# Scan loads placed over the convolution's buffers, with a lasting weight slot, fewer copies and evenly spread preparation steps

## The chip, the cores and the metric

The kernel runs on one core of one Trainium2 chip. A core has a matrix engine (PE, with its weight loads shown as PEld), a vector engine (DVE), a scalar engine (ACT), GpSimd (POOL) and a sync engine (SP) that here only issues transfers. Each engine works through its own instructions in the order fixed when the kernel is built, and waits where an instruction's inputs or its buffer are not ready. The metric is the device time of one execution in microseconds. Three runs of the kernel before took 1540.7, 1546.32 and 1547.51 us; their median is 1546.32.

## The reference

One layer of a diffusion backbone over 1024 latent tokens and 256 context tokens of width 1024. Cut to its course:

```python
px = modulate(rms_norm(x, norm1_w[i]), sh1, sc1) @ w_in[i]
pc = modulate(rms_norm(ctx, norm1_w[i]), csh1, csc1) @ w_in[i]
dn_c, s_ctx_f, s_ctx_b = gated_deltanet(pc[..., :DN_IN], ..., s_zero, s_zero)
dn_x, _, _ = gated_deltanet(px[..., :DN_IN], ..., s_ctx_f, s_ctx_b)
qx, kx, vx = na_qkv(px[..., DN_IN:], ...)
qc, kc, vc = na_qkv(pc[..., DN_IN:], ...)
na_x = neighborhood_attention(qx, kx, vx, kc, vc, na_rpb[i], rows)
x = x + g1 * (jnp.concatenate([dn_x, na_x], axis=-1) @ w_out[i])
x = x + g2 * swiglu(modulate(rms_norm(x, norm2_w[i]), sh2, sc2), w_ffn_in[i], w_ffn_out[i])
```

`gated_deltanet` convolves q, k and v over the sequence (five taps, then SiLU), normalises q and k, and runs a gated delta rule in chunks, forward and backward, each over the context first. Its output is normalised per head and multiplied by `silu(z)`. `neighborhood_attention` gives each latent query one softmax over a clamped 8 x 16 window of keys and all context keys.

## The kernel before

The work goes through four stages: the normalised, modulated tokens; the input projection as a list of jobs; the two scans, with the attention filled in between their steps; and the output projection with the feed-forward part, which holds more than half of the time and is not touched.

**Order.** Only the first stage's order is written out by hand. Everywhere else the program is built from Python generators, and the framework's scheduler orders the instructions of each engine when the kernel is built: by the place in the program, and by when it expects inputs and buffers to be ready. Its expectations are not the chip's times; the chip then keeps the order. SP's queue of transfers is ordered in the same way.

**The job list** (L1030 to L1039) is k0 to k3, z1, nk0 to nk2, nv0, nk3, q0 to q3, nq0 to nq3, v0, nv1, v1 to v3, z0. A `Block` (k, q, v with convolution; nk, nq without) computes 128 output columns for all tokens: eight steps of matmuls with split operands hh and hl (L405), then the evacuation by ACT into a raw tile `cr` (L453), the taps on DVE into `cacc` (L457, L461), SiLU on ACT (L468), and, one or two jobs later, `norm` and `finish`. For v, `finish` transposes `cacc` on PE (L527), scales it on DVE into `vt` (L531), and SP stores it to v_d (L535). For nk and nq, `norm` multiplies the squares with a block of ones in two or three segments (L492), each followed by Ln on ACT (L493), with two PSUM banks of the name "m". A `Wide` job (z, nv) takes 256 columns with the tokens as stationary operand (L595), tile by tile; its weights come in two halves through a single raw buffer `wraw` (load L586, cast on ACT L587, remainder on POOL L588) into a tile `zw`. z1, nv0 and nv1 take `zw` from a pool `zp` on the left side; z0 takes a tile of its own from a pool `sp1`, made where `zp`, `adp` and the preparation's pools have been closed. z0 writes its gate tiles `zg` into slots of the tag "kx" and stores them from ACT (L627). While z0 runs, PSUM is divided anew: it then has two banks for everything beside the attention.

**Beside the jobs** two backgrounds advance: `block_inverses` and `preps` (the chunks' triangular inverses and decay tables, kk, at, y), and `modulation`. A Block gives the first of them one step for each of its eight matmul steps, a Wide job two for each tile, and nv1 three. What is left is drained at the beginning of v3. The preparation's results go out by SP (L1010) to at_d and y_d, and its decay matmuls read the masks `mr` and a constant `mneg` (L968).

**Around the change's middle.** After nv1, SP copies the latent values within DRAM into the window layout vw_d, in 64 transfers of 32 rows (L1108). At the beginning of v3 the attention's pool `nw` is made and its first loads are issued: queries, keys (L260 to L263), context values, bias tiles (cleared by POOL, L271) and window values. The attention's generator `fill` is then advanced during z0 and the scans.

**The right side of the memory** is a stack of pools: the projection's weights `wpb`, the operands hh and hl in `hp` and `hp2`, and the convolution's pool `cp` (cacc, cr, kx, zt). After the last job it is reused in the same order by `wpf`, `arp`, then `sl` (three buffers of each of the scans' loads but v), a spacer, and `sw` (the scans' working tiles, and v). So `sl` lies mostly over the last of the operands hh and hl, and `sw` mostly over `cp`. The scans' loads are L1165; their first matmul is L1217.

Of the kernel before, what the change touches and what calls it, by code (L numbers as in the profile page):

```python
# [20 lines left out]
KT = 8  # L21
# [67 lines left out]
def hybrid(ctx, tc, a, dbg):  # L89
# [47 lines left out]
    mr = const("mr", [128, 5, 128], F32R)  # L137
    mneg = const("mneg", [128, 2, 128], F32R)

# [235 lines left out]
    with ExitStack() as bs:  # L375
# [32 lines left out]
        class Block:  # L408
# [64 lines left out]
            def norm(self):  # L473
# [8 lines left out]
                if kind == "q":  # L482
# [6 lines left out]
                    return  # L489
                for s0, n in self.segs:  # L490
                    p = bank()
                    pe.matmul(p[:, :n], M[C_BD2], r[:, s0:s0 + n], start=True, stop=True)  # L492
                    act.activation(r[:, s0:s0 + n], p[:, :n], AF.Ln, bias=b_eps, scale=1.0 / ND)  # L493
# [26 lines left out]
            def finish(self):  # L520
                kind, acc, i = self.kind, self.acc, self.i
                if kind in "kv":
                    vt = cp.tile([128, NCH, 128], F32, name="vt", tag="kx", bufs=3)
                    for g, m in ((0, 4), (4, 4), (8, 2)):
                        p = bank()
                        for c in range(m):
                            pe.transpose(p[:, c * 128:(c + 1) * 128], acc[:, (g + c) * 128:(g + c + 1) * 128], ident)  # L527
                        if kind == "k":
                            act.copy(vt[:, g:g + m].rearrange("p c d -> p (c d)"), p[:, :m * 128])
                        else:  # L530
                            dve.tensor_tensor(vt[:, g:g + m], p[:, :m * 128].rearrange("p (c d) -> p c d", d=128),  # L531
                                              SV[:, g:g + m, i:i + 1].to_broadcast([128, m, 128]), OP.mult)
                        yield
                    dst = v_d if kind == "v" else k_d
                    sp.dma_start(dst[:, i * 128:(i + 1) * 128].rearrange("(c p) d -> p c d", p=128), vt)  # L535
                if kind == "q":
# [27 lines left out]
        class Wide:  # L564


            def __init__(self, kind, half, zp):
                self.kind, self.half, self.zp = kind, half, zp
                self.n = 272 if kind == "z" and half else 256
                self.lasting = kind == "z" and not half  # L570

            def room(self):
                w = self.zp().tile([128, 2, KT, 256 if self.lasting else 272], F32R, name="zw", tag="zw")
                self.hi, self.lo = w[:, 0], w[:, 1]

            def prefetch(self):
                h2, n = 2 * self.half, self.n // 2
                src = a["w_nv"] if self.kind == "nv" else a["w_z%d" % self.half]
                if self.kind == "z":
                    h2 = 0  # L580
                if not self.lasting:
                    self.room()
                for i in range(2):
                    raw = wp.tile([128, KT, 136], F32, name="wraw", tag="wraw", bufs=1)
                    r, s = raw[:, :, :n], slice(i * n, i * n + n)
                    sp.dma_start(r, src[h2 + i])  # L586
                    act.copy(self.hi[:, :, s], r)  # L587
                    pool.tensor_tensor(self.lo[:, :, s], r, self.hi[:, :, s].bitcast(F32), OP.subtract)  # L588
# [10 lines left out]
            def tiles(self):  # L599
# [18 lines left out]
                for t in range(2, NCH):  # L618
                    p = self.wide(t, 0, self.n)
                    if half == 0:  # L620
                        if t % 4 == 2:
                            zg = cp.tile([128, NCH, 128], F32, name="zg", tag="kx", bufs=3)
                            zg = zg.rearrange("p a b -> p (a b)")[:, :1024]
                        act.copy(zg[:, (t - 2) % 4 * 256:(t - 2) % 4 * 256 + 256], p[:, :256])
                        if t % 4 == 1:
                            act.activation(zg, zg, AF.Silu)
                            act.dma_start(z_d[(t - 5) * 128:(t - 1) * 128, 0:256].rearrange("(c p) d -> p c d", p=128),  # L627
                                          zg.rearrange("p (c d) -> p c d", d=256))
                        yield
                        continue  # L630
# [13 lines left out]
        with ExitStack() as xs:  # L644
# [65 lines left out]
            with tc.manual_schedule(engines={mybir.EngineType.PE, mybir.EngineType.DVE, mybir.EngineType.Activation}):  # L710
# [30 lines left out]
                for k in range(1, KT):  # L741
# [12 lines left out]
                    if k == 5:  # L754
                        act.copy(mr[:, 4], ident)
                        for d in range(2):
                            act.mul(mneg[:, d], masks[:, d], -1.0e30)
                        act.copy(mr[:, 0:4], masks)

        cp = pools(bs, "cp", "right")  # L760
        late = ExitStack()
        adp = pools(late, "adp", "left")
        zpool = [pools(late, "zp", "left")]
        first_half = ExitStack()
        cpa = pools(first_half, "cpa", "left")
        WK = cpa.tile([128, 2, NU, 32], F32, name="WK", tag="WK")
        KKc = WK[:, 1]

        def zp():
            return zpool[0]  # L770

# [53 lines left out]
        def block_inverses():  # L825
            with ExitStack() as gs:
# [55 lines left out]
                for c in range(30, 0, -1):  # L882
# [5 lines left out]
                    if c % 2:  # L888
                        yield
                flat = N.rearrange("p b r c -> p b (r c)")  # L890
                dve.memset(flat[:P, :, 0:1024:33], 1.0)
# [137 lines left out]

        jobs = first + [Block("k", 2), Block("k", 3), Wide("z", 1, zp)]  # L1030
        inv = len(jobs)
        jobs += [Block("nk", i) for i in range(3)] + [Wide("nv", 0, zp), Block("nk", 3)]
        turn = len(jobs)
        jobs += [Block("q", i) for i in range(4)]
        later = len(jobs)
        queries = range(turn, later)
        jobs += [Block("nq", i) for i in range(4)] + [Block("v", 0), Wide("nv", 1, zp)]
        values = len(jobs) - 1
        jobs += [Block("v", i) for i in (1, 2, 3)] + [Wide("z", 0, zp)]  # L1039

# [11 lines left out]
        for n in range(2, len(jobs) + 2):  # L1052
# [7 lines left out]
            if n == len(jobs) - 2:  # L1060
                bg.drain()
                bg2.drain()
                late.close()
                sp1 = pools(middle, "sp1", "left")
                zpool[0] = sp1
                jobs[n + 1].room()
                fill = attention(pools(attn, "nw", "left", 2))
                next(fill)
# [8 lines left out]
            if isinstance(j, Wide):  # L1077
                for t, _ in enumerate(j.tiles()):
# [4 lines left out]
                    if t == 4 and nrm:  # L1083
# [5 lines left out]
                        nrm = None  # L1089
                    bg.step(3 if n == values else 2)  # L1090
            elif j:
                for k in range(KT):
                    j.mm([k])
                    if k >= 3:
                        next(fin, 0)
                    bg.step(1)
                    if n > inv + 4:
# [5 lines left out]
            if isinstance(j, Wide) and n == values:  # L1103
                vlat = nv_d[CT:].rearrange("(r c) d -> r c d", c=64)
                for cb in range(4):
                    for ch in range(4):
                        for r in range(4):
                            sp.dma_start(vw_d[r * 32:r * 32 + 32, :, cb, ch],  # L1108
                                         vlat[4 * ch + r, BLKS[cb]:BLKS[cb] + 32].rearrange("c (h d) -> c h d", d=128))
            if nrm:  # L1110
# [30 lines left out]

    with ExitStack() as gs:
        sl = pools(gs, "sl", "right", 3)
        shift(gs, "spad", "right", 16)
        sw = pools(gs, "sw", "right", 2)
        gs.callback(scan_psum.close)
# [14 lines left out]
        def load(d, c, near):  # L1161

            def tile_of(name, src):
                t = work(name, 3) if name == "v" else sl.tile([128, 4, 128], F32, name=name, tag=name)
                sp.dma_start(fl(t), src)  # L1165
# [612 lines left out]
```

## Time and profile before

| | us |
|---|---|
| median of three runs | 1546.32 |
| lowest, highest | 1540.7, 1547.51 |
| the profiled execution | 1549.54 |
| its span in the profile | 1547.5 |
| PE busy in it | 1479.8 |
| DVE, ACT, POOL busy | 994.3, 727.7, 233.6 |

The jobs run to about 595 us of the span, the scans with the attention to about 815, the output projection and the feed-forward part to the end. The profile gives, for each group of instructions, its line, engine, operation and operands, its count, busy time and mean duration, and the idle time of its engine just before it with what ended that idle time. Names like PEq, ACTq, SPq are an engine's queue of transfers and other instructions that do not compute. A strip of 40 digits cuts the span into equal slices of 38.7 us. In a list in order of time the first column is the start, the second the duration, and a bracket at the end tells how long the engine had stood and what released it.

### The profile page before, as it was taken

What the parts mean: (1) busy time and instruction counts of PE and PEld (TensorE: products, weight loads), DVE (VectorE), ACT (ScalarE), POOL (GpSimd) and SP (SyncE); (2) the same over time, 40 slices, a digit from 0 to 9 for tenths busy, and PEclk for the clock granted to TensorE, in tenths of its full rate; (3) what the DMA queues carried; (4) which work ended last, traced back from release to release, by engine and by line L of the source; (5) the groups of instructions that cost most, each with busy time, mean ns of one, the idle gap of its engine ahead of it and who ended that gap; (6) DMA issues with size and microseconds to landing.
All of it is one profiled execution on the core that took longest, in us unless ns stands there. A gap on an engine that the chain in (4) does not pass through costs nothing. (4 is left out here: it accounts for less than half of the span.)

```text
span 1547.5 us, 23963 instructions
## 1 busy us (share of the span) xinstructions
PE 1479.8 (96%) x8702; PEld 1235.2 (80%) x8702; DVE 994.3 (64%) x1712; ACT 727.7 (47%) x1404; POOL 233.6 (15%) x286
## 2 busy tenths in 40 slices
PE   6999999899989978999999999999999999999998
PEld 3788787678778867888887878888888888888887
DVE  5774497675554543777986469866665556599652
ACT  5442552635764235666773166333333334354440
POOL 1154500733554010111210000000000000000000
PEclk9999999999999979999999999999999999999999
DMA  9274221577556467899637502632323324698742
GB/s 389 64 217 133 67 72 63 163 212 241 182 169 212 130 174 237 283 288 261 220 102 255 208 34 82 211 102 103 103 102 103 109 100 159 231 381 279 244 144 82
DMA packets 204118, 267.35 MB, mean 173 GB/s; under 512 B 16736, under 2 KB 114528, under 8 KB 202976
## 3 DMA queue, kind: packets, MB, share of 16 engines
q1 hardware_dynamic: 198480, 261.07, 51.7%
q10 hardware_dynamic: 5520, 4.76, 0.9%
q8 instruction: 68, 1.11, 0.3%
q14 instruction: 50, 0.41, 0.1%
HBM read 201.02 MB, written 68.94 MB: 174 GB/s over the span
## 5 line engine op out<-in xcount | busy, mean ns | idle before, releaser
L405 PE MATMUL blk<-hh,whi 128*128 128x512 f32 (+1 forms) x410 | 123.4, 395 | 2.3 <-ACT kk L550 1.4
L1415 ACT CAST uhi<-wq 128x512 fp32r<-128x512 f32 x101 | 61.0, 622 | 133.5 <-issue 84.6
L1415 ACT CAST uhi<-ws 128x512 fp32r<-128x512 f32 x91 | 53.9, 621 | 147.3 <-PE ps L1354 92.9
L405 PE MATMUL blk<-hl,whi 128*128 128x512 f32 (+1 forms) x410 | 116.8, 377 | 0.3 <-DVE hl L707 0.3
L595 PE MATMUL blk<-zw,hh 128*128 128x256 f32 (+1 forms) x576 | 115.0, 293 | 1.3 <-ACT kk L550 1.1
L405 PE MATMUL blk<-hh,wlo 128*128 128x512 f32 (+1 forms) x410 | 114.7, 377 | 0.6 <-POOL wlo L200 0.6
L1416 DVE TENSOR_TENSOR ulo<-wq,uhi 128x512 fp32r<-128x512 f32 x101 | 67.4, 687 | 59.1 <-ACT uhi L1415 34.0
L1354 PE MATMUL ps<-hT,uhi 128*128 128x512 f32 x336 | 103.7, 390 | 0.0
L1354 PE MATMUL ps<-hT,ulo 128*128 128x512 f32 x336 | 103.5, 389 | 0.0
L1354 PE MATMUL ps<-lT,uhi 128*128 128x512 f32 x336 | 103.4, 389 | 0.0
L595 PEld LDWEIGHTS blk<-zw,hh 128*128 128x128 f32 x576 | 92.8, 192 | 5.2 <-ACT kk L550 1.4
L1354 PE MATMUL ps<-hB,uhi 128*128 128x512 f32 x288 | 89.2, 391 | 0.6 <-ACT hB L1529 0.6
L1354 PE MATMUL ps<-lB,uhi 128*128 128x512 f32 x288 | 88.7, 389 | 0.4 <-DVE lB L1530 0.4
L1354 PE MATMUL ps<-hB,ulo 128*128 128x512 f32 x288 | 88.7, 389 | 0.0
L405 PEld LDWEIGHTS blk<-hh,wlo 128*128 128x128 f32 x410 | 72.6, 192 | 15.3 <-POOL wlo L200 0.9
L405 PEld LDWEIGHTS blk<-hl,whi 128*128 128x128 f32 x410 | 72.4, 191 | 14.5 <-DVE hl L707 0.8
L405 PEld LDWEIGHTS blk<-hh,whi 128*128 128x128 f32 x410 | 69.4, 194 | 18.2 <-issue 4.5
L595 PE MATMUL blk<-zw,hl 128*128 128x256 f32 (+1 forms) x288 | 83.2, 289 | 0.0
L1354 PEld LDWEIGHTS ps<-lT,uhi 128*128 128x128 f32 x336 | 63.1, 188 | 13.1
L1354 PEld LDWEIGHTS ps<-hT,ulo 128*128 128x128 f32 x336 | 63.1, 188 | 13.1
L1354 PEld LDWEIGHTS ps<-hT,uhi 128*128 128x128 f32 x336 | 62.9, 188 | 13.0
L200 POOL TENSOR_TENSOR wlo<-wraw,whi 128x1024 fp32r<-128x1024 f32 x18 | 44.7, 2485 | 179.2 <-ACT whi L199 160.7
(359 smaller groups left out, 3540.5 us busy)
## 6 DMA issues: line engine op xcount, KB each, us to landing
wq<-w_fo SPq DMA_DIRECT2D x99, 256.0 KB, 4.2
wq<-w_gu SPq DMA_DIRECT2D x88, 256.0 KB, 2.9
wad<-wa SPq DMA_DIRECT2D x64, 256.0 KB, 4.4
bt<-rpb SPq DMA_DIRECT2D x64, 192.0 KB, 3.8
t_d<-g SPq DMA_DIRECT2D x22, 512.0 KB, 3.6
fr<-t_d SPq DMA_DIRECT2D x44, 256.0 KB, 5.0
f_d<-g SPq DMA_DIRECT2D x33, 256.0 KB, 2.1
fr<-f_d SPq DMA_DIRECT2D x33, 256.0 KB, 3.8
```

What stands on the lines that cost most here:

```text
L200: lo_engine.tensor_tensor(o, r, h.bitcast(F32), OP.subtract)
L405: pe.matmul(o, ww[:, k], xx[k][:, s], start=k == 0 and j == 0, stop=k == KT - 1 and j == 2)
L595: pe.matmul(p[:, :c1 - c0], x[k][:, s], ww[:, k, c0:c1], start=k == 0 and j == 0, stop=k == KT - 1 and j == 2)
L1354: pe.matmul(o, w[wi][:, k], x[xi][:, k], start=first and k == 0 and j == 0, stop=k == n - 1 and j == 2, skip_group_check=True)
L1415: act.copy(hi, self.raw[key])
L1416: dve.tensor_tensor(lo, self.raw[key], hi.bitcast(F32), OP.subtract)
```

## The change

Eight edits, told apart:

1. **vw_d**: 16 transfers of 4 x 32 rows in place of 64 of 32 rows.
2. **v_d stores** are issued by ACT in place of SP.
3. **The weight slot**: `sp1` is made at the beginning and lasts; all Wide jobs take `zw` from it, z0 too. `zp` is gone.
4. **mneg** moves out of the constants into `adp`, and is made from `mr` after the first stage.
5. **norm**'s third segment takes a bank of the name "pr", the preparation's pair.
6. **Gate tiles** `zg` take a slot of the raw tiles' tag "cr" in place of "kx".
7. **Steps**: nv1 gives two per tile, as other Wide jobs; Blocks from nq0 on give ten in place of eight; `block_inverses` has two empty steps more before it sets the diagonal.
8. **The scans' pools** change places: `sw` first, `sl` last, and v's three buffers move to `sl`. So `sl` lies over `cp`, and `sw` over the last of the operands.

```diff
-    mneg = const("mneg", [128, 2, 128], F32R)
...
-                for s0, n in self.segs:
-                    p = bank()
+                for j, (s0, n) in enumerate(self.segs):
+                    p = bank("pr" if j == 2 else "m")
...
-                    sp.dma_start(dst[:, i * 128:(i + 1) * 128].rearrange("(c p) d -> p c d", p=128), vt)
+                    (act if kind == "v" else sp).dma_start(dst[:, i * 128:(i + 1) * 128].rearrange("(c p) d -> p c d", p=128), vt)
...
-                self.lasting = kind == "z" and not half
...
-                w = self.zp().tile([128, 2, KT, 256 if self.lasting else 272], F32R, name="zw", tag="zw")
+                w = sp1.tile([128, 2, KT, 272], F32R, name="zw", tag="zw")
...
-                if not self.lasting:
-                    self.room()
+                self.room()
...
-                            zg = cp.tile([128, NCH, 128], F32, name="zg", tag="kx", bufs=3)
-                            zg = zg.rearrange("p a b -> p (a b)")[:, :1024]
+                            zg = cp.tile([128, T], F32, name="zg", tag="cr", bufs=2)
+                            zg = zg[:, :1024]
...
-                        for d in range(2):
-                            act.mul(mneg[:, d], masks[:, d], -1.0e30)
                         act.copy(mr[:, 0:4], masks)
...
         late = ExitStack()
+        sp1 = pools(middle, "sp1", "left")
         adp = pools(late, "adp", "left")
-        zpool = [pools(late, "zp", "left")]
+        mneg = adp.tile([128, 2, 128], F32R, name="mneg", tag="mneg")
+        for d in range(2):
+            act.mul(mneg[:, d], mr[:, d].bitcast(F32), -1.0e30)
...
                     if c % 2:
                         yield
+                yield
+                yield
                 flat = N.rearrange("p b r c -> p b (r c)")
...
                 late.close()
-                sp1 = pools(middle, "sp1", "left")
-                zpool[0] = sp1
-                jobs[n + 1].room()
...
-                    bg.step(3 if n == values else 2)
+                    bg.step(2)
...
-                    bg.step(1)
+                    bg.step(1 + (n >= later and k in (2, 6)))
...
-                        for r in range(4):
-                            sp.dma_start(vw_d[r * 32:r * 32 + 32, :, cb, ch],
-                                         vlat[4 * ch + r, BLKS[cb]:BLKS[cb] + 32].rearrange("c (h d) -> c h d", d=128))
+                        sp.dma_start(vw_d[:, :, cb, ch].rearrange("(r c) h d -> r c h d", c=32),
+                                     vlat[4 * ch:4 * ch + 4, BLKS[cb]:BLKS[cb] + 32].rearrange(
+                                         "r c (h d) -> r c h d", d=128))
...
-        sl = pools(gs, "sl", "right", 3)
-        shift(gs, "spad", "right", 16)
         sw = pools(gs, "sw", "right", 2)
+        shift(gs, "spad", "right", 16)
+        sl = pools(gs, "sl", "right", 3)
...
-                t = work(name, 3) if name == "v" else sl.tile([128, 4, 128], F32, name=name, tag=name)
+                t = sl.tile([128, 4, 128], F32, name=name, tag=name)
```

More of the change, by code (lines that the diff above doesn't have):

```diff
@@ L564, in hybrid, with __init__ @@
         class Wide:
-            def __init__(self, kind, half, zp):
-                self.kind, self.half, self.zp = kind, half, zp
+            def __init__(self, kind, half):
+                self.kind, self.half = kind, half
                 self.n = 272 if kind == "z" and half else 256
-                self.lasting = kind == "z" and not half
             def room(self):
-                w = self.zp().tile([128, 2, KT, 256 if self.lasting else 272], F32R, name="zw", tag="zw")
+                w = sp1.tile([128, 2, KT, 272], F32R, name="zw", tag="zw")
                 self.hi, self.lo = w[:, 0], w[:, 1]
@@ L767, in hybrid @@
         KKc = WK[:, 1]
-        def zp():
-            return zpool[0]
         def decay_tables(gp):
@@ L1028, in preps @@
                 flush(tick[0] + 2)
-        jobs = first + [Block("k", 2), Block("k", 3), Wide("z", 1, zp)]
+        jobs = first + [Block("k", 2), Block("k", 3), Wide("z", 1)]
         inv = len(jobs)
-        jobs += [Block("nk", i) for i in range(3)] + [Wide("nv", 0, zp), Block("nk", 3)]
+        jobs += [Block("nk", i) for i in range(3)] + [Wide("nv", 0), Block("nk", 3)]
         turn = len(jobs)
@@ L1036, in hybrid @@
         queries = range(turn, later)
-        jobs += [Block("nq", i) for i in range(4)] + [Block("v", 0), Wide("nv", 1, zp)]
+        jobs += [Block("nq", i) for i in range(4)] + [Block("v", 0), Wide("nv", 1)]
         values = len(jobs) - 1
-        jobs += [Block("v", i) for i in (1, 2, 3)] + [Wide("z", 0, zp)]
+        jobs += [Block("v", i) for i in (1, 2, 3)] + [Wide("z", 0)]
         def blk(n):
@@ L1142, in hybrid @@
     with ExitStack() as gs:
+        sw = pools(gs, "sw", "right", 2)
+        shift(gs, "spad", "right", 16)
         sl = pools(gs, "sl", "right", 3)
-        shift(gs, "spad", "right", 16)
-        sw = pools(gs, "sw", "right", 2)
         gs.callback(scan_psum.close)
```

## The prediction

> **What bounds the kernel now.** I read the page first, for which engine is full and where its clock drops; then the busy time of single stretches; then the matrix engine in order of time; then the queues that feed it.
>
> ```profile
> span 1547.5 us, 23963 instructions
> PE 1479.8 (96%) x8702; PEld 1235.2 (80%) x8702; DVE 994.3 (64%) x1712; ACT 727.7 (47%) x1404; POOL 233.6 (15%) x286
> PE   6999999899989978999999999999999999999998
> PEclk9999999999999979999999999999999999999999
> ```
>
> PE is busy 96% of the span, so the change, which takes no matmul away, can only win PE's idle time (1547.5 - 1479.8 = 67.7 us) and time at a low clock. Both strips show one weak place, the fifteenth slice (542 to 580 us). There the last convolution block (v3) ends and the last wide job (z0) begins.
>
> ```profile
> 548.50:565.60 17.10, 6.01 (x28) 3.84 (x27) 14.62 (x20) 8.27 (x14) 4.79 (x3) 0.61 0.93 258
> 565.60:569.40 3.80, 3.80 (x18) 3.80 (x19) 1.13 (x3) 0.40 (x1) 0.17 (x1) 0.50 0.72 212
> 569.40:595.00 25.60, 25.55 (x218) 24.44 (x218) 4.55 (x9) 8.12 (x14) 0.31 (x1) 1.00 0.36 99
> ...
> 547.75 0.75 PE L405 MATMUL blk<-hh,wlo 128*128 128x256 f32 x3
> 553.04 0.58 PE L303 MATMUL sc<-kh,qs 128*128 128x256 f16 x2 [4.54 <-DMA kh<-nk_d]
> ...
> 559.55 0.37 PE L303 MATMUL sc<-kh,qs 128*128 128x256 f16 x1 [4.11 <-DVE mx L305]
> ...
> 563.07 0.66 PE L314 MATMUL sc<-cst,bt 128*128 128x128 f32 x2 [2.29 <-DVE bt L309]
> ...
> 565.57 0.80 PE L595 MATMUL blk<-zw,hh 128*128 128x256 f32 x2
> ```
>
> A window row gives its length, busy time and count of PE, weight loads, DVE, ACT and POOL, then granted clock, DMA share and GB/s. In 17.1 us PE is busy 6.01 us, at a clock of 0.61. v3's last matmul (L405) ends at 548.50; z0 (L595) runs in earnest from 565.57. What stands between is attention work that was filled in, with three waits (4.54, 4.11, 2.29). They are symptoms: had z0's weights been ready, PE would have had work. So I follow the weights.
>
> ```profile
> 517.64 2.38 POOL L200 TENSOR_TENSOR wlo<-wraw,whi 128x1024 fp32r<-128x1024 f32 x1 [17.36 <-PE pr L998]
> 538.13 1.07 POOL L271 MEMSET bt<- 128x256 f32 x4 [18.11 <-DMA y_d<-y]
> 550.50 2.34 POOL L588 TENSOR_TENSOR zw<-wraw,zw 128x1024 fp32r<-128x1024 f32 x1 [11.30 <-ACT zw L587]
> 563.15 2.37 POOL L588 TENSOR_TENSOR zw<-wraw,zw 128x1024 fp32r<-128x1024 f32 x1 [10.31 <-ACT zw L587]
> ...
> 548.13 1.35 ACT L453 COPY cr<-blk 128x256 f32<-128x256 f32 x3 [5.77 <-PE blk L405]
> 549.35 1.07 ACT L587 CAST zw<-wraw 128x1024 fp32r<-128x1024 f32 x1
> 558.64 1.27 ACT L468 ACTIVATE cacc<-cacc 128x1280 f32<-128x1280 f32 x1 [8.22 <-DVE cacc L461]
> ...
> 550.51 8.04 DVE L461 SCALAR_TENSOR_TENSOR cacc<-cr,cw,cacc 128x255 f32<-128x255 f32 x6
> ...
> 495.88 36.09 SPq L1108 DMA_DIRECT2D vw_d<-nv_d  x53
> 533.18 2.42 SPq L1010 DMA_DIRECT2D y_d<-y  x4
> 535.68 0.61 SPq L586 DMA_DIRECT2D wraw<-w_z  x1
> 545.47 0.37 SPq L535 DMA_DIRECT2D v_d<-vt  x1
> 546.65 1.16 SPq L262 DMA_DIRECT2D kh<-nk_d  x1
> ...
> 555.34 0.60 SPq L586 DMA_DIRECT2D wraw<-w_z  x1
> ...
> wraw<-w_z SPq DMA_DIRECT2D x2, 512.0 KB, 5.3
> ```
>
> Backwards from 565.57: POOL's second remainder (L588) ends at 563.15 + 2.37 = 565.52. Its raw half was loaded only at 555.34, because there is one raw buffer and POOL's first remainder left it at 552.84. The first half was loaded at 535.68, though the buffer was free at 517.64 + 2.38 = 520.02: SP was issuing 53 small copies into vw_d for 36.09 us. The preparation's last y_d stores stand behind those copies too, the clearing of the bias tiles (538.13) waits for them, and SP then stands until 545.47 for v1's transposed tile, with attention's keys (546.65) queued behind it. The place is bound by SP's queue, 36 us long and twice blocked.
>
> **The change, part by part.**
>
> *The copies into vw_d* go from 64 DMAs to 16 of four times the size. An issue costs 36.09/53 = 0.68 us, so the 53 of the long run become about 13, 9 us, and SP is free near 505 instead of 532. The price of one larger copy has no row; its bounds are 0.68 us (per DMA) and 2.7 us (per run moved, nothing gained). Nearest is v_d<-vt, ten times the bytes in 0.37 us: I take per DMA. Then the first half of z0's weights loads from 520.0: landing +5.3, cast +1.07, remainder +2.34, second load +5.3, cast +1.07, remainder +2.37 gives 537.5, 11 us before PE wants it. *The lasting slot*: z0's weights now take the slot of nv1's, whose job is long over; it no longer has to wait until the preparation's pools close. That costs nothing, and the cover is the same 11 us. So PE goes from v3 straight to z0. Of the 17.1 us, the work in it stays, at full clock 6.01 x 0.61 = 3.7 us: **-13.4**. The 3.80 us behind it at clock 0.50 become 1.9: **-1.9**. Late next are v3's taps on DVE (to 558.55) and its Silu (to 559.9). If a z0 copy stood behind that Silu in ACT's order, PE would fill its two banks and stop: z0's eight tiles take 25.6 us, 3.2 each, so from 548.5 + 6.4 = 554.9 to 559.9 and a copy of 0.4, 5.4 us. Bounds 0 and +5.4; the nearest row is the job nv1, where the copy of a tile ran ahead of the Silu that waited for DVE:
>
> ```profile
> 450.24 0.37 ACT L605 COPY zt<-blk 128x256 f32<-128x256 f32 x1
> ...
> 455.68 1.27 ACT L468 ACTIVATE cacc<-cacc 128x1280 f32<-128x1280 f32 x1
> ...
> SPq L535 <- DVE vt L531: 21.6, 2, 12.6
> PE m L492 <- ACT cr L493: 5.3, 4, 1.4
> PE m L492 <- ACT cr L493: 4.0, 3, 1.4
> PE m L897 <- DVE N L891: 2.9, 1, 2.9
> PE pr L987 <- ACT y L1001: 2.5, 1, 2.5
> PE pr L987 <- ACT kk L990: 2.3, 1, 2.3
> ```
>
> I take **+2**.
>
> *v_d stores on ACT's queue.* Four issues of 0.37 us move; ACT is 47% busy. SP no longer stands for them (21.6 us in two waits), so attention's loads follow the y_d stores; ACT stands instead if a store comes before its tile. Behind it are then PSUM copies. Bounds 0 and the rival below; I take 0, since z0's eight tiles give other work before it.
>
> *norm's third bank.* L492's third matmul waits for Ln to empty the first of two banks; with a bank of the other pair it doesn't. All four waits are 5.3; three of them (4.0) lie before 250 us, ahead of any preparation that uses those banks: **-4.0**; bounds 0 and -5.3.
>
> *Two empty steps* before the diagonal is set: PE's wait for N (2.9) gets two more steps of other matmuls ahead of it. Whether two cover it no row shows; I take it whole, **-2.9**; bounds 0 and -2.9.
>
> *Even steps.* From nq0 to nv1's end there were 4x8 + 8 + 30 = 70 steps, now 4x10 + 10 + 20 = 70: the same work, earlier. It may thin the waits in nv1 (2.5 and 2.3) or bring such into the nq blocks: 0, bounds -4.8 and +4.8.
>
> *mneg* is made later, from mr, two ACT instructions, hidden under ACT's idle time, long before its first reader; each is half the size of the 0.37 us copy above, so without cover under 0.8 us. *Gate tiles in the convolution's raw slots*: the older raw is free before the first gate tile, the newer at 558.55: 0.
>
> *The scans' loads over the convolution's buffers.* Before, they lay over operands that the last z0 tile reads; now over buffers whose last user is the second gate tile's store or v3's v_d store.
>
> ```profile
> 598.01 0.37 ACTq L627 DMA_DIRECT2D z_d<-zg  x1
> ...
> 602.13 0.32 SPq L1165 DMA_DIRECT2D v<-v_d  x1
> ...
> z_d<-zg ACTq DMA_DIRECT2D x2, 512.0 KB, 4.5
> PE ps L1217 <- DMA y<-y_d: 2.3, 2, 1.6
> 500.00:525.00 25.00, 25.00 (x181) 20.21 (x181) 10.52 (x16) 7.84 (x14) 2.66 (x2) 1.00 0.34 95
> ```
>
> That store lands at 598.01 + 4.5 = 602.5; the first load was issued at 602.13 anyway. Same place relative to z0's end: 0. At best PE's 2.3 us of waits for y go; at worst a later landing costs as much.
>
> **Sum**: -13.4 - 1.9 + 2 - 4.0 - 2.9 = -20.2. The profiled execution took 1549.54 (span 1547.5 and 2.0 around it), so 1529.3. The median of the three runs, 1546.32, is 3.2 below that execution; the same difference gives **1526**. Bounds together: -15.3 - 5.3 - 2.9 - 4.8 - 2.3 = -30.6 and -15.3 + 5.4 + 4.8 + 2.3 = -2.8. Not all ends come together; the likeliest case alone covers 1514 to 1536.
>
> **Rivals.**
>
> 1. *The weights land early, ACT takes them late.* ACT's order is fixed when the kernel is built; the cast at 549.35 came behind L453 though its half was there near 541. If both casts keep such places, the second behind v3's Silu (558.64 + 1.27 = 559.9), then 559.9 + 1.07 + 2.37 = 563.4: 2.2 won instead of 15.3, with the 6.9 of the banks and steps. 1537. For it: that 5.77 us idle. Against: the order follows expected readiness, which moves with SP.
>
> 2. *The large copies crowd the transfer engines.* The last row: 25 us of copying at share 0.34 on 16 engines is 136 engine-us for 25/0.68 = 36.8 copies, 3.7 each, so 14.8 for a large one. Its slowest dimension goes from 32 rows to 4. If that number says how many engines share it, it takes 3.7 us on four, and 13 of them 48 us, to 544; loads issued behind land after that. z0's first half is then ready at 544 + 1.07 + 2.34 = 547.4, the second at +5.3 + 1.07 + 2.37 = 556.1: 9.4 us won there, half clock kept, 6.9 elsewhere, 2 lost. 1532. The Trainium skill, "DMA: Bandwidth & Descriptors", Rules for kernel authors, says just this: an outermost dimension of c < 16 keeps a DMA on at most c engines. No copy in this trace has so few rows outermost. For another end: copies of early rows may start before 495.
>
> 3. *ACT inherits SP's wait* (the slower side). Four stores stand in ACT's order before their tiles; behind them are the copies that free PE's two banks. Two tiles of 3.2 us hide up to 6.4 us of a wait: from there on PE stops. SP's own 21.6 us, moved to ACT in two pieces, cost 21.6 - 12.8 = 8.8, and the first piece holds z0's cast, so the 15.3 stay lost; with 6.9 won and 1.9 of half clock after each of two stops, 1546.3 + 8.8 - 6.9 + 3.8 = 1552. Against: SP reached these stores early because it had nothing ready; ACT has work.
>
> 4. *It doesn't do what it says*: a copy's issue costs by the run, SP stays at 532 and the casts too; only the 6.9 come. 1539.5.
>
> **How the numbers follow.** Forecast 0.56, rivals in order 0.14, 0.12, 0.11, 0.07. The runs shown spread 0.4%, so I count 0.5% as the least that can be told: 1538.6 and 1554.1. Faster: 0.56 + 0.12 + 0.10 of rival 1 + 0.01 of rival 4 = 0.79. Same: 0.04 of rival 1, 0.06 of rival 4, 0.04 of rival 3: 0.14. Slower: 0.07 (rival 3 with waits 2 us longer or more). The range 1513 to 1541 takes in the forecast's own range, rivals 1, 2 and 4, and leaves out rival 3 and the far end of the sum, under 2 in 10.
>
> **What would show it.** Right: the vw_d copies take under 15 us of SP; both w_z loads are issued before 540; L595 begins within 2 us of v3's last L405, at full clock; L492 waits under 2 us in all; PE's busy share is above 97%. Wrong: L587's second cast behind L468 (rival 1), loads issued near 505 to 520 landing after 540 (rival 2), a gap before L595 that ends on an ACT copy behind a v_d issue (rival 3). The forecast as a whole is wrong if z0 begins on time and the span doesn't fall: then the gap has moved to the scan's start near 595.

## The result, and the profile after

The changed kernel took 1591.57 us (median of 4 runs, 1588.18 to 1591.76) beside 1546.91 for the kernel before (4 runs): a ratio of 1.0288, 95% interval 1.0253 to 1.0324, so some 45 us slower where 20 us faster were forecast. The profiled execution took 1588.18, its span is 1586.3, 38.8 longer than that of before.

The head of the changed kernel's page, and two of its strips:

```profile
span 1586.3 us, 23907 instructions
PE 1486.5 (94%) x8702; PEld 1241.0 (78%) x8702; DVE 991.5 (63%) x1712; ACT 731.1 (46%) x1407; POOL 235.7 (15%) x286
...
PE   6999998999789918899999999999999999999999
...
PEclk9999998999999958999999999999999999999999
```

The busy times of the engines are nearly those of before; PE's idle time has grown. The weak place is where it was, a slice of 40 us with PE busy for less than two tenths of it. The next fences show it by windows (columns as in the prediction), then in PE's own order of time.

```profile
553.16:580.71 27.55, 4.40 (x49) 3.42 (x48) 8.68 (x13) 2.87 (x5) 2.29 (x8) 0.54 0.42 135
580.71:599.87 19.16, 5.86 (x26) 3.79 (x26) 4.95 (x11) 6.63 (x11) 5.76 (x7) 0.50 0.89 252
599.87:628.80 28.93, 28.88 (x235) 27.77 (x234) 5.47 (x12) 8.68 (x15) 0.86 (x2) 0.94 0.41 116
```

```profile
552.41 0.75 PE L404 MATMUL blk<-hh,wlo 128*128 128x256 f32 x3
576.20 4.51 PE L995 MATMUL pr<-y,kk 128*32 128x32 f32 x48 [23.04 <-POOL y L974]
587.62 0.58 PE L302 MATMUL sc<-kh,qs 128*128 128x256 f16 x2 [6.91 <-DMA kh<-nk_d]
...
594.56 0.37 PE L302 MATMUL sc<-kh,qs 128*128 128x256 f16 x1 [4.61 <-DVE mx L304]
...
599.87 0.80 PE L592 MATMUL blk<-zw,hh 128*128 128x256 f32 x2
...
646.51 1.16 PE L1211 MATMUL ps<-v,y 128*128 128x128 f32 x8 [1.07 <-DMA y<-y_d]
```

(The line numbers have moved by 1 to 7: L404, L592, L995, L1211 are L405, L595, L998, L1217 of before.) v3's last matmul ends at 553.16 and z0 runs in earnest from 599.87: the gap of 17.1 has become 46.7, at about half clock, and it now holds preparation work (L995) that before had ended at 520.7 (here and below the end of the preparation and of z0 is the start of its last matmul). With 4.7 us that v3 ends later (548.50 before) this is 34.3 of the 38.8. Another 5.4 come at the scans' start: z0's last matmul begins at 628.8, the scans 17.7 us later (before 594.9, and 12.3). z0 itself and all behind it give 0.9 of these 39.7 back. What SP, POOL and ACT did meanwhile:

```profile
504.59 63.47 SPq L1101 DMA_DIRECT2D vw_d<-nv_d  x15
568.16 3.29 SPq L1007 DMA_DIRECT2D y_d<-y  x2
...
573.83 0.62 SPq L583 DMA_DIRECT2D wraw<-w_z  x1
...
590.29 0.99 SPq L583 DMA_DIRECT2D wraw<-w_z  x1
...
641.41 0.33 SPq L1159 DMA_DIRECT2D v<-v_d  x1
...
574.88 2.65 POOL L974 COPY y<-xc 32x128 f32<-32x128 f32 x8 [49.74 <-DMA y_d<-y]
...
550.13 0.38 ACTq L534 DMA_DIRECT2D v_d<-vt  x1
...
635.29 0.37 ACTq L534 DMA_DIRECT2D v_d<-vt  x1
...
629.33 0.42 DVE L530 TENSOR_TENSOR vt<-m,SV 128x256 f32<-128x256 f32 x1 [3.14 <-PE m L526]
```

Fifteen large copies held SP for 63.47 us, where 53 small ones had held it for 36.09. Behind them stood y_d's stores (568.16); POOL could not refill the y tiles until these had left (49.74), PE waited 23.04 for that, and z0's weights were loaded at 573.83 and 590.29 (before 535.68 and 555.34). So SP's queue, which the change was to free at 505, was free at 568.

The waits of SP's queue between 495 and 620, the durations of the copies' issues (shortest, median, longest in ns), the first copy's issue, and a window among the last ones:

```profile
SPq L1101 <- DMA v_d<-vt: 24.8, 1, 24.8
...
L1101 SPq DMA_DIRECT2D vw_d<-nv_d x16: 592/2951/3236, 478.4 to 565.1; - x16
...
478.45 0.75 SPq L1101 DMA_DIRECT2D vw_d<-nv_d  x1
...
554.00:566.00 12.00, 0.00 (x0) 0.00 (x0) 6.96 (x9) 1.41 (x2) 0.00 (x0) 0.56 0.25 75
```

In a run of copies an issue took 2.95 us. The first copy, which left alone at 478.45, took 0.75, and the one behind the pause 0.59: a large copy is cheap to issue until others stand ahead of it. The window from 554 to 566 holds no transfers but these copies; the share of the 16 transfer engines is 0.25. That is four engines' worth, the size of the copies' slowest dimension: the Trainium skill ("DMA: Bandwidth & Descriptors", Rules for kernel authors), weighed in rival 2, says that such a transfer stays on at most four, and the trace agrees. That each issue in a run holds SP's queue for this long is rival 2's picture; its 3.7 us for one was an estimate, 2.95 is the measured one. And one copy stood 24.8 us for a v_d store, with which it shares no data.

### The profile page after: what moved, and what is told of

Read it like the earlier page. It is cut to its first block, busy times and chain, and to the rows that moved or that the text cites. A ratio compares the mean times of both kernels' runs of the same rounds, so it can differ in the third digit from the quotient of the medians.

```text
span 1586.3 us, 23907 instructions
## 1 busy us (share of the span) xinstructions
PE 1486.5 (94%) x8702; PEld 1241.0 (78%) x8702; DVE 991.5 (63%) x1712; ACT 731.1 (46%) x1407; POOL 235.7 (15%) x286
## 5 line engine op out<-in xcount | busy, mean ns | idle before, releaser
L404 PE MATMUL blk<-hh,whi 128*128 128x512 f32 (+1 forms) x410 | 122.3, 391 | 1.4 <-ACT kk L549 1.4
L404 PE MATMUL blk<-hl,whi 128*128 128x512 f32 (+1 forms) x410 | 117.3, 381 | 0.3 <-DVE hl L704 0.3
L592 PE MATMUL blk<-zw,hh 128*128 128x256 f32 (+1 forms) x576 | 114.5, 293 | 1.2 <-ACT kk L549 1.1
L404 PE MATMUL blk<-hh,wlo 128*128 128x512 f32 (+1 forms) x410 | 115.0, 377 | 0.6 <-POOL wlo L199 0.6
L592 PEld LDWEIGHTS blk<-zw,hh 128*128 128x128 f32 x576 | 93.4, 194 | 4.6 <-ACT kk L549 1.4
L404 PEld LDWEIGHTS blk<-hh,wlo 128*128 128x128 f32 x410 | 72.7, 193 | 15.0 <-POOL wlo L199 0.9
L404 PEld LDWEIGHTS blk<-hl,whi 128*128 128x128 f32 x410 | 72.8, 193 | 14.5 <-DVE hl L704 0.8
L404 PEld LDWEIGHTS blk<-hh,whi 128*128 128x128 f32 x410 | 69.9, 193 | 17.3 <-issue 4.0
L592 PE MATMUL blk<-zw,hl 128*128 128x256 f32 (+1 forms) x288 | 82.8, 288 | 0.0
L304 DVE CUSTOM_DVE_ANT_0 bt<-sc,bt 128x640 f32<-128x640 f32 x64 | 52.6, 821 | 33.5 <-DMA bt<-rpb 14.1
```

Of the source, the lines that this page charges most:

```text
L304: dve.tensor_tensor_reduce(bt, sc[:, u * 640:u * 640 + 640], bt, -1.0, 3.0e38, OP.add, OP.min, m[:, 0:1])
L404: pe.matmul(o, ww[:, k], xx[k][:, s], start=k == 0 and j == 0, stop=k == KT - 1 and j == 2)
L592: pe.matmul(p[:, :c1 - c0], x[k][:, s], ww[:, k, c0:c1], start=k == 0 and j == 0, stop=k == KT - 1 and j == 2)
```

## The experiments

Letters of theories are given anew in each group. All ratios are to the kernel before, run on the same chip.

| run | edit | median us | ratio (95%) |
|---|---|---|---|
| small_copies | after, 64 small copies | 1555.56 | 1.0017 (0.9997 to 1.0036) |
| v_on_sp | after, v_d stores on SP | 1570.22 | 1.0123 (1.0092 to 1.0154) |
| small_and_v_on_sp | after, both | 1557.74 | 1.0036 (1.0016 to 1.0056) |
| before_large_copies | before, 16 large copies | 1557.09 | 1.0049 (1.0023 to 1.0076) |
| large_old_steps | after, old steps | 1583.52 | 1.0227 (1.0197 to 1.0257) |
| small_old_steps | after, small copies, old steps | 1553.0 | 1.0027 (1.0008 to 1.0045) |
| steps_alone | before, new steps | 1556.99 | 1.0049 (1.0031 to 1.0067) |
| v_store_alone | before, v_d stores on ACT | 1554.69 | 1.0032 (1.0013 to 1.0050) |
| bank_alone | before, third bank | 1552.19 | 1.0019 (1.0006 to 1.0033) |
| early_weights_act | see below | 1545.22 | 0.9980 (0.9965 to 0.9995) |
| early_weights_pool | see below | 1542.12 | 0.9952 (0.9925 to 0.9979) |
| early_copies_pool | see below | 1550.71 | 1.0003 (0.9988 to 1.0018) |
| v1_store_on_sp | after, v1's store on SP | 1580.92 | 1.0192 (1.0163 to 1.0220) |
| early_weights_large | early_weights_pool, large copies | 1575.78 | 1.0157 (1.0131 to 1.0182) |
| early_weights_no_bank | early_weights_pool, no third bank | 1542.26 | 0.9939 (0.9913 to 0.9964) |

**Copies or store.** The two edits that touch SP's queue were undone one by one and together, and the copies were put alone into the kernel before.

```diff
-                        sp.dma_start(vw_d[:, :, cb, ch].rearrange("(r c) h d -> r c h d", c=32), ...)
+                        for r in range(4):
+                            sp.dma_start(vw_d[r * 32:r * 32 + 32, :, cb, ch], ...)
```
```diff
-                    (act if kind == "v" else sp).dma_start(dst[...], vt)
+                    sp.dma_start(dst[...], vt)
```

> The changed kernel with the copies into vw_d as before (64 of 32 rows). Theory A (the large copies, 4 rows outermost, hold SP's queue, one of them also waiting 24.8 us for a v_d store on ACT's queue): the run of copies is back near 36 us, PE's 23 us wait for the y tile is gone, 1525 to 1548. Rival B (the v_d stores on ACT are enough to block SP, whatever the copies' size): PE still stands over 10 us between v3 and z0, 1560 to 1590. Rival C (steps, slot and pools cost the time): 1575 to 1592, with the gap elsewhere.

> The changed kernel with the v_d stores back on SP. Theory A (copies at fault by their own length, 3 us each): no 24.8 us wait, but the copies still hold SP for 16 x 3 = 48 us, to about 553; PE still stands some 5 to 15 us before z0: 1555 to 1575. Rival B (the wait across the queues is the whole loss): 1525 to 1550. Rival C: 1575 to 1592.

> The changed kernel with both undone: what the other six edits do alone. Theories A and B: within 10 us of the kernel before, 1535 to 1556, with a gap before z0 like the one before (about 14 us), less L485 and N waits. Rival C: still above 1570.

> The kernel before with only the copies merged into 16. Theory A: SP is held for 13 to 16 times 3 us, so 3 to 12 us longer than before, the y_d stores and z0's first load as much later: 1550 to 1562. If four engines and SP's queue don't matter without the store on ACT (rival B): 1538 to 1550. If the large copies are the whole loss by themselves: above 1575.

Theory A, the copies, has the order right: without them 2.7 of the 2.9% are gone, and alone they cost 0.5% on the kernel before. v_on_sp and before_large_copies fell into its ranges of time, though in v_on_sp PE stood idle for 24.7 of the 35.5 us between v3 and z0, where it expected 5 to 15. But its range for small_copies (up to 1548) was too low by 8 us, that for small_and_v_on_sp by 2, and the two edits do not add up: on top of the six others the copies cost 0.9% with the stores on SP (1.0123 against 1.0036) and 2.7% with the stores on ACT (1.0288 against 1.0017). The surplus of 1.8%, 28 us, belongs to the two together, and so does the wait of 24.8.

**The wait of 24.8.** The built program shows on what a transfer waits. Every transfer, SP's and ACT's alike, takes one of eight counters, and whoever takes a counter again waits until the last transfer on it has landed. Of the changed kernel's order on the two queues, the copies about the place and v1's store (at its place in ACT's order):

```
SP   vw_d<-nv_d  waits counter 1
SP   vw_d<-nv_d  waits counter 2
SP   vw_d<-nv_d  waits counter 4
...
SP   vw_d<-nv_d  waits counter 3
ACT  v_d<-vt     waits counter 3, DVE
```

Counter 3 is missing in the copies' first turn: v1's store has it. v1_store_on_sp moves this one store (`i != 1` in ACT's condition).

> The changed kernel with v1's v_d store alone back on SP; the large copies, the other three stores on ACT and all else stay. Theory C (in the changed kernel one copy stood 24.8 us although its data lay ready: the built order lets it wait for the transfer counter that v1's store on ACT held, and that store waited for its tile): the copies now run on without a wait over 5 us, y_d's stores leave near 545 instead of 568, PE's wait of 23.0 us for y falls below 10, and the time is 1562 to 1576, as with all four stores on SP (1570). Rival (the large copies or the transfer engines by themselves cause the pause): the wait stays over 15 us at the copies or behind them, 1582 to 1593.

SP's queue and PE in v1_store_on_sp:

```profile
506.16 42.63 SPq L1101 DMA_DIRECT2D vw_d<-nv_d  x15
548.90 3.29 SPq L1007 DMA_DIRECT2D y_d<-y  x2
...
557.52 0.64 PE L995 MATMUL pr<-y,kk 128*32 128x32 f32 x8 [2.75 <-POOL y L974]
```

The fifteen copies now take 42.63 instead of 63.47, y_d's stores leave at 548.90, PE's wait for POOL's y is 2.75 instead of 23.04. So the pause came from the shared counter: the copy stood for a store that ACT could issue only when v1's tile was done (550.13). The time, 1581, is 5 us above the expected range and by the ratios some 15 below the changed kernel, so this one store makes about half of the surplus of 28; the rest stays with the other three stores. With the pause gone, SP is still held to 548.90, and z0's weights leave at 554.56 and 579.78, against 535.68 and 555.34 in the kernel before.

**The steps.** The old steps were put back beside large and small copies, and the new ones put alone into the kernel before.

```diff
-                    bg.step(2)
+                    bg.step(3 if n == values else 2)
...
-                    bg.step(1 + (n >= later and k in (2, 6)))
+                    bg.step(1)
```

> The changed kernel with the preparation's steps as before (three a tile in nv1, one a k in the blocks, no two empty steps); large copies and the v_d store on ACT stay. Theory D (from nq2 to nv1's end the new spread makes 50 steps where the old made 54, and two more are empty, so the last rounds of the preparation meet the held SP queue; PE then waits 23.0 us for y): with the old steps the last matmul of the preparation (L995 of the changed kernel) ends before 545 instead of 580.3, PE's wait of 23.0 us shrinks below 8, z0 begins between 568 and 585, and the time is 1558 to 1578. Theory E (the held queue alone costs the 45 us, the steps play no part): 1586 to 1593, the wait for y stays above 18 us.

> The changed kernel with 64 small copies and the old steps; the v_d store on ACT, the third bank, the lasting slot, the gate tiles and the scans' pools stay. Theory D: the preparation ends 20 us or more earlier than with small copies and the new steps (547.2), v3 ends by 551, PE's wait of 5.7 for N is back at 2 to 4, and the ratio to before is 0.994 to 0.999. Theory E (steps play no part): the ratio stays at 1.000 to 1.004, as with small copies and the new steps.

> The kernel before with the new steps alone, the two empty ones included. My forecast: -2.9 us, ratio 0.997 to 0.999. Theory D: the preparation ends later than 520.7 by 15 us or more, new waits for y in the blocks between 360 and 465 (L964 and L995 of the changed kernel) with half clock beside them, the wait for N does not shrink: ratio 1.002 to 1.007. Theory E: 0.999 to 1.001.

PE in large_old_steps:

```profile
579.84 0.58 PE L302 MATMUL sc<-kh,qs 128*128 128x256 f16 x2 [31.40 <-DMA kh<-nk_d]
```

With the old steps the preparation ended at 520.6 instead of 580.3, as D had it, and the wait of 23.0 was gone. Yet the run of copies still held SP for 65.11 us, PE stood 31.40 in one piece for attention's keys in the same queue, and of the 45 us only some 10 came back (1.0227). The time lies between the ranges of D and E: D had the order of events right, E the price. The held queue carries most of the loss, and the late preparation mainly chose what PE stood for. Alone, the steps cost 0.5%, as D said. PE's waits in steps_alone, for N in 250 to 360 and then the three longest in 360 to 500:

```profile
PE m L899 <- DVE N L893: 2.9, 1, 2.9
...
PE pr L969 <- ACT y L1003: 5.0, 2, 2.6
PE pr L969 <- DVE y L1002: 2.6, 1, 2.6
PE pr L1000 <- ACT kk L992: 2.3, 2, 1.7
```

The two empty steps bought nothing (2.9 for N, as before), and the preparation ended at 552.7 instead of 520.7: while the queries are not done, steps for later chunks are empty, so only the steps from nq2 on count, 8 + 8 + 8 + 30 = 54 before and 10 + 10 + 10 + 20 = 50 after. Beside small copies and the other edits the steps' cost cannot be told from nothing (1.0017 against 1.0027). In small_old_steps the preparation ended at 518.4 and v3 at 546.2, as D said, and still the ratio is E's; the wait for N stayed at 5.7, so it is not the steps' either. ACT's queue and ACT there:

```profile
543.19 0.38 ACTq L534 DMA_DIRECT2D v_d<-vt  x1
543.61 1.05 ACT L584 CAST zw<-wraw 128x1024 fp32r<-128x1024 f32 x1 [3.56 <-DVE vt L530]
```

z0's first half had been loaded at 530.72, but its cast stood behind v1's store, which waited for its tile. That is rival 3 of the prediction, at z0's cast; it led to the versions further down.

**The store and the bank alone.** `sp.dma_start` becomes ACT's for v in the one, `bank()` becomes `bank("pr" if j == 2 else "m")` in the other.

> The kernel before with the v_d store on ACT's queue alone. My forecast counted it at 0 (0.999 to 1.001). Rival 3 of the forecast (ACT inherits SP's wait): ratio 1.002 to 1.006, with a gap before z0 that ends on an ACT copy. Theory F (seen in the runs so far): the waits for attention's keys at 553 shrink (4 us won), but v3's store is issued some 5 us after its tile is done, behind attention's work in ACT's order, and the first scan load waits for it: the scan begins 16 to 18 us after z0's end instead of 12.3; both together 0.999 to 1.002.

> The kernel before with the third bank in norm alone. My forecast: L492's waits go, -4.0 us, ratio 0.996 to 0.999. Theory B (the norms end earlier, but the inverses' chain on DVE (N) ends when it did, so PE waits there instead): L492's four waits (5.3) are gone, the wait for N grows from 2.9 to 5 to 7, ratio 0.999 to 1.002.

The end of v3 in v_store_alone, on DVE, ACT's queue and SP's:

```profile
595.55 0.42 DVE L531 TENSOR_TENSOR vt<-m,SV 128x256 f32<-128x256 f32 x1 [3.18 <-PE m L527]
...
601.52 0.37 ACTq L535 DMA_DIRECT2D v_d<-vt  x1
...
607.30 0.38 SPq L1165 DMA_DIRECT2D v<-v_d  x1
```

The tile is done at 595.97; ACT issues its store 5.5 us later, behind attention work that stands first in its order; the first scan load goes out at 607.30. On SP the store had left at 596.43 and the load at 602.13. Theory F holds as to the place; its size, 0.32%, lies above the 0.2% it allowed, for the 4 us that it expected to win at the keys did not come: PE stood 7.07 us for the bias tiles instead, and z0 ran in earnest from 565.82 (before 565.57). Rival 3 of the prediction had the engine right and the place wrong: not z0's start, the scans' start.

In bank_alone L492's waits are gone. The row for N's wait, and N's products (first and last start) in the kernel before and in bank_alone:

```profile
PE m L897 <- DVE N L891: 5.7, 1, 5.7
...
L897 PE MATMUL m<-cst,N x32: 275/341/341, 257.7 to 264.1; 80*128 80x80 f32 x32
...
L897 PE MATMUL m<-cst,N x32: 335/341/400, 256.7 to 264.2; 80*128 80x80 f32 x32
```

Of the 4 us that PE won ahead of it, it stood 2.8 us longer for N. N's products begin only 1 us earlier and end where they did, so there the gain is given back. The ratio is 1.0019; what cost the little more no run here shows. In early_weights_no_bank N's wait is back at 2.9 and the norm's four waits at 5.3, as theory B says, but the time could not be told from that of early_weights_pool (0.9939 and 0.9952).

**z0's weights early.** These are the changed kernel with small copies, old steps, v3's store on SP (v0 to v2 on ACT), and z0's loads put into the program right behind v3's, which the lasting slot allows. early_weights_pool has z0's casts on POOL too; early_copies_pool also issues each 16 copies right behind the tile of nv1 that completes their rows.

```diff
-            if n + 1 < len(jobs):
+            if n + 1 < len(jobs) and not (n + 1 == len(jobs) - 1):
                 jobs[n + 1].prefetch()
+            if n == len(jobs) - 3:
+                jobs[n + 2].prefetch()
...
-                    act.copy(self.hi[:, :, s], r)
+                    if self.kind == "z" and not self.half:
+                        pool.tensor_copy(self.hi[:, :, s], r)
+                    else:
+                        act.copy(self.hi[:, :, s], r)
```

> The changed kernel with small copies, the old steps, v3's v_d store on SP (v0 to v2 on ACT), and z0's two weight loads put into the program right behind v3's weights, a job earlier than now; the casts stay on ACT. Theory G (what holds z0 is the chain of its two weight halves: load, cast on ACT in an order that stands behind other work, remainder on POOL, then the second load into the one raw buffer): the second load is issued before 545 instead of 550, but its cast still stands behind the evacuation of v3 (L452, near 548); z0 begins in earnest at 552 to 556 instead of 557 to 562; scan begins about 12.5 us after z0's end; ratio 0.993 to 0.999. Rival H (the gap only moves, to attention's DVE work and to the scan's start): ratio 0.999 to 1.003.

> As early_weights_act, and z0's casts are made by POOL ahead of its remainders (a cast took POOL 1.24 us), so that ACT's order no longer matters. Theory G: the chain is 527 + 5.3 + 1.24 + 2.4, then 5.3 + 1.24 + 2.4 again: ready near 545 to 548, z0 begins within 3 us of v3's last matmul with no attention work between them; ratio 0.988 to 0.995. Rival H: z0 begins on time but the ratio stays at 0.998 to 1.003 because the time comes back behind it.

> As early_weights_pool, and the small copies of each four rows (16 copies) are issued right after the tile of nv1 that completes them instead of all after the last tile. Theory G: 20 us or more of SP's queue are free earlier, y_d's stores and the weight loads leave before 520, weights ready near 540; as v3 ends near 546 the time is that of early_weights_pool, 0.987 to 0.995. Rival (the copies now stand between the preparation's loads, whose tiles PE waits for in nv1): new waits of 3 us or more for kk, xc or at in 460 to 500, ratio 0.995 to 1.003.

Theory G holds for the first two: the one is 0.2% faster than the kernel before, the other 0.5%, at the slow end of its range; they are the first versions that beat it. SP, POOL, PE and ACT of early_weights_pool:

```profile
522.34 0.61 SPq L583 DMA_DIRECT2D wraw<-w_z  x1
...
531.47 0.60 SPq L583 DMA_DIRECT2D wraw<-w_z  x1
...
537.01 2.42 POOL L588 TENSOR_TENSOR zw<-wraw,zw 128x1024 fp32r<-128x1024 f32 x1
...
539.00 0.74 PE L404 MATMUL blk<-hh,wlo 128*128 128x256 f32 x3
540.82 0.36 PE L595 MATMUL blk<-zw,hh 128*128 128x256 f32 x1 [1.08 <-issue]
...
549.33 0.39 PE L595 MATMUL blk<-zw,hh 128*128 128x256 f32 x1 [2.59 <-ACT zg L624]
...
547.75 1.27 ACT L467 ACTIVATE cacc<-cacc 128x1280 f32<-128x1280 f32 x1 [7.03 <-DVE cacc L460]
548.92 0.63 ACT L624 COPY zg<-blk 128x256 f32<-128x256 f32 x2
```

The weights are ready at 539.43, and PE goes from v3 to z0 within 1.1 us: the picture of the forecast, here. What is late next is what the forecast named: z0's first copies stand behind v3's Silu (547.75) in ACT's order, its two banks are full, and PE waits 2.59 (forecast: 2). This profiled execution, 1529.39, is the fastest of its nine; why it lies 13 us below their median no run here settles. early_copies_pool is no faster than the kernel before: its preparation ended at 544.5 instead of 511.9, and z0's second half, behind the last y_d stores, left only at 546.81. That the copies between the preparation's loads delayed it fits this but is not shown; none of the waits of 3 us that the rival named appeared.

**Large copies with the rest put right, and no third bank.**

> As early_weights_pool (casts on POOL, z0's loads put in behind v3's, old steps), with the large copies instead of the small. Theory A (what the large copies cost is SP's queue, held about 3 us for each): w_z's first load leaves 15 us or more later than in early_weights_pool, z0 begins 10 to 30 us after v3, ratio to before 1.004 to 1.020, that is 1 to 2.5% over early_weights_pool. Rival (once nothing urgent stands behind them the copies are free): ratio 0.993 to 0.998.

> As early_weights_pool without norm's third bank. Theory B (the bank's gain is given back at N, where PE then waits 5.7 in one piece and its clock halves): the wait for N is back at 2.9 or less, L492's waits come back, and the ratio is 0.001 to 0.003 below that of early_weights_pool. My forecast: 0.002 to 0.003 above it.

v3's end and z0's start on PE in early_weights_large:

```profile
548.00 0.75 PE L404 MATMUL blk<-hh,wlo 128*128 128x256 f32 x3
584.34 0.58 PE L595 MATMUL blk<-zw,hh 128*128 128x256 f32 x1 [35.59 <-POOL zw L585]
```

SP was held for 65.81 us by fifteen copies, 25.8 of it again for a v_d store's counter; w_z's first load left at 568.62 instead of 522.34. With that pause the large copies cost 2.1% here, 32 us: even where the weights are asked for early, the held queue is the cost. z0 began 36 us after v3, later than the 10 to 30 expected, since the counter's pause came back.

## Why the prediction was wrong

**What bounds the kernel** was read rightly: SP's queue ahead of z0. Three of the four versions that bring z0's weights forward with small copies win, and every version with large copies, which hold the queue longer, loses.

**The copies** are where it failed: "The price of one larger copy has no row; its bounds are 0.68 us (per DMA) and 2.7 us (per run moved, nothing gained). Nearest is v_d<-vt, ten times the bytes in 0.37 us: I take per DMA." Per DMA holds for a copy that goes alone (0.75). In a run of fifteen the measured issue is 2.95 us, past the upper bound, so merging four copies of 0.68 (2.7 together) saves nothing. v_d<-vt was the wrong neighbour: it is ten times as large but goes alone and has 128 rows outermost; the copies follow one another and have four. Which of the two counts for how much is open, as no copy of this size with more rows outermost was tried. With 2.95 the terms of -13.4 and -1.9 are not won: z0 starts 34.3 later in the changed kernel. In the kernel before with large copies alone the row is

```profile
502.90 42.39 SPq L1107 DMA_DIRECT2D vw_d<-nv_d  x15
```

SP is free at 545.29 instead of 531.97. Of the 13.3 us, 6.3 are the longer run and 7.0 its later beginning; one of the 16 large copies had left ahead of it, where eleven of the 64 small ones had.

**Rival 2** had mechanism and place: four engines, 3.7 us each, SP's loads behind them "to 544". It failed behind that, as it let z0's first half land by 544. In the kernel before with large copies alone y_d's stores stood first and w_z left at 551.10 and 565.80, with 10.6 us of PE's time for attention's keys; +0.5%, not a gain of 9.4. A queue held longer delays all that stands in it, and I priced one transfer. **Rival 4**, a price by the run, had the nearest price (2.7), but left SP free at 532 and added 6.9 of gains that did not come.

**v_d on ACT, "I take 0"**: 0.3% alone, at the scans' start, by ACT's order. Beside the large copies 1.6%, 26 us (1.0288 against 1.0123), of which v1's store, by the shared counter, makes 15. No part of the prediction had a mechanism by which a store on one queue stops another queue; rival 3 came nearest.

**Even steps, "70 now 70: the same work, earlier"**: the sum counted steps that do nothing. It is 54 to 50, and later; 0.5% alone.

**norm's bank, -4.0**: the waits went as said, and the gain was lost at N, whose wait I had covered with **the two empty steps, -2.9**. Both stand on the same wait: N is made by DVE, and was ready only 1 us earlier. The terms were added as if each ended a wait of its own; together they gave 2.8 us more of waiting for N and no gain.

**z0's copies behind the Silu, +2**: right, 2.59 measured in early_weights_pool, where the weights came in time. **The scans' pools, 0**: the first product behind the attention lasted 24.4 us in the changed kernel instead of 23.4, a microsecond lost there; that the new pools cost it is not shown, as they were not tried alone. **mneg, gate tiles, the lasting slot** were not tried alone either; the slot is what lets z0's loads move up.

**Of the five signs** named, only L492's waits went. The copies took 63.47 instead of under 15, the loads left at 573.83 and 590.29 instead of before 540, z0 began 46.7 behind v3 instead of 2, and PE's share is 94%.

## What to carry to other kernels

Merging transfers into fewer larger ones can save nothing: here four small issues of 0.68 us became one of 2.95. Before a merged transfer is priced, find a row with as few rows outermost and in a run of its kind, not one that goes alone, and list everything queued behind. Moving a transfer to another queue does not free the first if the two share completion counters: a transfer that waits for its data then stops both. Two terms of a sum that end at one engine's result are not to be added, and steps of a background count only when they do something.

## What was not expected of the hardware

In a run of 256 KB copies with four rows outermost each issue lasted 2.95 us, while a quarter of the sixteen transfer engines was busy, against 0.68 us for a quarter of the bytes with 32 rows; the same copy alone took 0.75. One queue stood 24.8 us for a transfer of another queue without shared data (25.8 in early_weights_large), and not when that one store was moved.
